# The second product of the second MLP with activations stationary: 512 weight columns moving, tokens on partitions

## The chip, the cores and the metric

The kernel runs on one core of a Trainium2 chip. The time is device microseconds of one execution; the figures given are the median of three runs and their spread. The trace is of one profiled execution, and its times count from the start of its span.

## What is computed

A trunk of two layers over 16 learned meta tokens and 256 real tokens, width 2048, all in float32: RWKV-7 time mixing, an MLP, gated linear attention (GLA), a second MLP, and a final norm. What the change touches is the end:

```python
def rms_norm(x, g, eps=NORM_EPS):
    y = x * lax.rsqrt(jnp.mean(x * x, axis=-1, keepdims=True) + eps)
    return y * g

def sq_relu_mlp(x, w1, w2):          # w1: 2048 x 8192, w2: 8192 x 2048
    h = jax.nn.relu(x @ w1)
    return (h * h) @ w2
...
    h = h + sq_relu_mlp(rms_norm(h, norm_mlp[i]), mlp_w1[i], mlp_w2[i])
return rms_norm(h, norm_f)[:, N_META:]
```

## The kernel before

The residual stream `hres` lies in SBUF as 128 partitions x 16 tiles x 272 tokens: features on partitions, tokens along the free axis. In the second MLP only the 256 real tokens are worked on.

**Weights.** They come from HBM in loads of 512 KB (128 partitions x 1024 float32), all issued on SP's queue (L132, tile `raw`, 3 buffers). Each is split in two: ScalarE casts it to a rounded part `hi` (L140), VectorE subtracts to get the rest `lo` (L141); `hi` and `lo` have 2 buffers each. These three steps carry a priority 2000 instructions ahead of their place in the program, so that the scheduler, which writes down a fixed order for each engine, puts them before other work that is ready at the same time. Activations are split in the same way. A product keeps hi x hi, hi x lo and lo x hi.

**Products.** A load holds 8 stationary tiles of 128x128. `projw` (L185 to L202) makes a pair of matmuls for each: behind the hi weights 512 columns move (256 tokens of the hi activations and 256 of the lo ones), behind the lo weights 256 columns (L196, L197). `mm3` (L163 to L165) does the same with three matmuls of 256 or 272 columns. The moving operand is read interleaved (`weave`). The result has features on partitions and accumulates in a PSUM bank of the tag `pj`, which has two banks. Other tags are `pm` (1), `pt` (2), `pry` (1) and `pu` (2).

**The MLP.** The hidden width 8192 is worked through in 4 blocks of 2048. `up(b)` makes 16 hidden tiles: a projection of 2 loads, the two halves joined (L206, L207), relu and scaling by the norm (L272), square (L275), split (L277, L278). `down(b)` projects the block onto 16 output tiles, 2 loads each, and two adds on VectorE put them into `hres` (L213). The order is up 0, up 1, down 0, up 2, down 1, up 3, down 2, down 3. The last output tile of the last block goes through `mm3`.

**The end.** While the last block goes down, `last` (L1307) squares each finished tile, sums the squares over tiles and multiplies the tile by `norm_f`. Then a product with ones sums over partitions (L1323), Ln and Exp give the norm's factor for each token (L231, L232), six products apply it, one of them on GpSimd (L1328), and six transfers on SP's queue write the output (L1330).

Two other places of the program serve as measures. At the start, 13 matmuls of 512 columns run on a constant tile, to have TensorE busy (L382). In the GLA and the RWKV layer, float32 transposes of 64 rows by 64 columns run in clusters on TensorE, two at a time on the two halves of the partitions (L1231, L745). L225 is a projection of plain float32 without a split.

Of the kernel before, what the change touches and what calls it, by code (L numbers as in the profile page):

```python
# [10 lines left out]
F32 = mybir.dt.float32  # L11
F32R = mybir.dt.float32r
AF = mybir.ActivationFunctionType
ALU = mybir.AluOpType
# [4 lines left out]
P = 128  # L19
D = 2048  # L20
KT = D // P
NMETA = 16
SEQ = 256
T = NMETA + SEQ
TP = 288
FF = 4 * D
NHB = FF // D
HEAD = 64
NG = 4
C = 64  # L30
NC4 = 4
DECAY = float(np.exp(-0.5))
NORM_EPS = 1e-6
# [13 lines left out]
GAPS = [(4, 2), (4, 2), (4, 2), (4, 3), (5, 5)]  # L47

MARK = [120, 170, 244, 302]

OUTQ = [0, 1, 4, 5]
OUTA = [4, 5, 6, 7, 12, 13, 14, 15]
# [2 lines left out]
class Kern:  # L55
# [203 lines left out]
    def mlp(self, layer, x, rstd, hres, off, done):  # L259
        nc, tc, ap = self.nc, self.tc, self.ap  # L260
        n = T - off
        w1, w2 = ap[f"mlp_w1_{layer}"], ap[f"mlp_w2_{layer}"]
        with ExitStack() as es:
            hp = es.enter_context(tc.tile_pool(name=f"hid{layer}", bufs=1, side="right", reuse_waits="tile"))

            def up(b):
                hid = []
                for f in range(KT):
                    src = [w1[b * KT + f, i] for i in range(2)]
                    ps = self.joined(hp, self.projw(src, x)) if n == SEQ else self.proj(src, x, n)  # L270
                    z = self.t(hp, [P, T], "z", 2)[:, :n]
                    nc.vector.scalar_tensor_tensor(out=self.two(z), in0=ps, scalar=0.0, in1=self.two(rstd), op0=ALU.max,  # L272
                                                   op1=ALU.mult)
                    s = self.t(hp, [P, T], "s", 2)[:, :n]
                    nc.scalar.activation(s, z, AF.Square)  # L275
                    ht = self.t(hp, [P, 2, T], "h", 2 * KT, F32R)
                    nc.scalar.copy(ht[:, 0, :n], s)  # L277
                    nc.vector.tensor_tensor(out=ht[:, 1, :n], in0=s, in1=ht[:, 0, :n].bitcast(F32), op=ALU.subtract)  # L278
                    hid.append(ht)
                return hid  # L280

            def down(b, hid):
                for f in range(KT):
                    src = [w2[f, 2 * b + i] for i in range(2)]
                    one = n != SEQ or (b, f) == (NHB - 1, KT - 1)
                    self.addto(hres[:, f, off:], [self.proj(src, hid, n)] if one else self.projw(src, hid))
                    if b == NHB - 1:
                        done(f)

            hid = up(0)  # L290
            for b in range(1, NHB):
                nxt = up(b)
                down(b - 1, hid)
                hid = nxt
            down(NHB - 1, hid)


    def rwkv(self, done):
# [228 lines left out]
        def scores(b, c, e):  # L527
            BK, AR = BKs[c > 1], ARs[c > 1]
            n, np = (C, 4) if c < NC4 else (32, 8)
            o = 128 * (c % 2) if c < NC4 else 256  # L530
            cs = slice(o, o + 2 * n)

            pv = [self.ptr().rearrange("p (h m) -> p h m", h=np)[: 2 * n, :, : 2 * n] for _ in range(2)]
            for p in range(np):
                for q in range(2):
                    rows = slice(64 * q, 64 * q + 64)
                    nc.tensor.matmul(pv[q][:, p], BK[rows, 4 * e + p, cs], AR[rows, 4 * e + p, cs], start=True, stop=True)
            dst, mk = (AMs[c > 1][:, c % 2, 8 * e : 8 * e + 8], self.maskA) if c < NC4 else (AMrs[0], self.maskR)
            for q in range(2):
                tt(dst[:, q::2], pv[q], mk.unsqueeze(1).to_broadcast([2 * n, np, 2 * n]))  # L540

            for rows, x in blocks(c, slice(8 * e, 8 * e + 8) if c < NC4 else slice(16)):
                with tc.high_priority(offset=4000):
                    nc.sync.dma_start(sysd[b][rows].rearrange("h s t -> s h t"), x)
# [418 lines left out]
        def until(n):  # L963
            R(n - ran[0])

        def some(it, n):
            for _ in range(n):
                next(it, None)
# [21 lines left out]
        with tc.manual_schedule(engines={ENG.PE}):  # L990
# [5 lines left out]
            for g in range(2):  # L996
                last = nothing
                if g:
# [7 lines left out]
                    last = norm(1)  # L1006
                until(MARK[2 * g])
                some(inv, 99)
# [19 lines left out]
                for c in range(5):  # L1028
                    if c == 2:
                        R(8)  # L1030
                        some(inv, 99)
                        if g == 0:
                            scores(2, 0, 0)
                        until(MARK[2 * g + 1])
                        m = merge(2 * g + 1)
# [243 lines left out]
@with_exitstack  # L1279
def trunk(ctx, tc, ap):  # L1280
    K = Kern(ctx, tc, ap)
    nc = tc.nc
    out, hres = ap["out"], K.hres
    st = {}

    def operand(gname, off, pool):
        def f(kt):
            if kt == 0:
                p = pool()
                st["x"] = [K.t(p, [P, 2, T], "x", KT, F32R) for _ in range(KT)]  # L1290
                st["acc"] = K.t(K.sp, [P, T], "acc")
            with tc.high_priority(offset=3000) if kt == KT - 1 else ExitStack():
                K.prep(K.sp, kt, hres[:, kt, off:], gname, st["x"][kt], st["acc"], T - off)
        return f

    def x2():
        K.x2p = K.sp = ctx.enter_context(tc.tile_pool(name="x2", bufs=1, side="right", reuse_waits="tile"))
        return K.x2p

    K.rwkv(operand("norm_mlp0", 0, x2))  # L1300
    rstd = K.accstd(K.sp, st["acc"], T)
    K.mlp(0, st["x"], rstd, hres, 0, operand("norm_mix1", 0, lambda: K.xp))
    rstd = K.accstd(K.sp, st["acc"], T)
    K.gla(st["x"], rstd, hres, operand("norm_mlp1", NMETA, lambda: K.xp))
    rstd = K.accstd(K.sp, st["acc"], SEQ)

    def last(kt):  # L1307
        if kt == 0:
            st["acc"] = K.t(K.sp, [P, T], "acc")
        h = hres[:, kt, NMETA:]  # L1310
        if kt < KT - 1:
            K.sqacc(K.sp, kt, h, st["acc"], SEQ)
        else:
            st["sq"] = K.t(K.sp, [P, T], "sq")[:, :SEQ]
            nc.scalar.activation(st["sq"], h, AF.Square)  # L1315
        nc.scalar.mul(h, h, K.vec("norm_f", kt))

    fp = ctx.enter_context(tc.tile_pool(name="fin", bufs=1, side="right"))
    fin = K.t(fp, [P, KT - 2, SEQ], "fin")
    K.mlp(1, st["x"], rstd, hres, NMETA, last)  # L1320
    ss = K.pm()[:, :SEQ]
    for i, x in enumerate((st["acc"][:, :SEQ], st["sq"])):
        nc.tensor.matmul(ss, K.ones, x, start=i == 0, stop=i == 1)  # L1323
    rstd = K.rstd_from(K.sp, ss, SEQ, 1.0 / D, NORM_EPS, "acc")
    for a, b in ((0, 1), (14, 16), (1, 3), (3, 6), (6, 10), (10, 14)):
        h = hres[:, a:b, NMETA:]
        y = fin[:, a:b] if b < KT else h
        (nc.gpsimd if b == KT else nc.vector).tensor_tensor(out=y, in0=h, in1=rstd.unsqueeze(1).to_broadcast([P, b - a, SEQ]),  # L1328
                                                           op=ALU.mult)
        nc.sync.dma_start(out[:, a:b], y)  # L1330


def _tiles(w):
    k, f = w.shape
    return np.ascontiguousarray(w.reshape(k // 1024, 8, P, f // P, P).transpose(3, 0, 2, 1, 4)).reshape(
        f // P, k // 1024, P, 1024)


def _pad(w, cols):
# [82 lines left out]
```

## Time and profile before

| | |
|---|---|
| median of 3 runs | 2378.53 us (2377.47 to 2379.18) |
| span of the profiled execution, its own time | 2375.3 us |
| TensorE matmuls busy | 2344.9 us, 19849 instructions |
| VectorE busy | 1607.3 us, 2701 instructions |
| ScalarE busy | 1259.7 us, 2005 instructions |
| moved by DMA | 449.20 MB |

The span runs from the first to the last instruction that the profiler recorded. Busy time is the time in which at least one instruction of the engine was under way; matmuls overlap each other, so a matmul's own duration is longer than the step from one to the next. PEld are the weight loads of TensorE. Register, branch, semaphore and DMA-issuing instructions are not counted as busy.

### The profile page before, as it was taken

The numbers are of one execution on the slowest core, as the hardware profiler recorded it, in microseconds if no ns is written. First come the engines' busy times: TensorE is split into PE (matmuls) and PEld (weight loads), VectorE is DVE, ScalarE is ACT, GpSimd is POOL, SyncE is SP. The second block draws the span as 40 slices with busy tenths as digits, with TensorE's granted clock in tenths as the row PEclk, the third lists the DMA queues.
The fourth block names the chain that finished last, engine by engine and source line by source line (L and its number), as shares of the span: only waits on it lengthen the run. The fifth ranks groups of instructions, "written<-read, shape, count | busy, mean of one in ns | idle before, by whom it ended". The sixth has DMA issues, their size and how long they took to land. (4 is left out here: it accounts for less than half of the span.)

```text
span 2375.3 us, 48373 instructions
## 1 busy us (share of the span) xinstructions
PE 2344.9 (99%) x19849; PEld 2224.1 (94%) x19849; DVE 1607.3 (68%) x2701; ACT 1259.7 (53%) x2005; POOL 13.6 (1%) x38
## 2 busy tenths in 40 slices
PE   9999999999999999999999999999999999999998
PEld 8888888889999999999999999999999999999997
DVE  8869986848555555555556777767666666666666
ACT  6478645566555345345345556645555445445444
POOL 0000000000000000000000000000000000000000
PEclk9999999999999999999999999999999999999999
DMA  6469754535555555555555655456565666666664
GB/s 214 155 198 310 245 159 145 144 98 180 186 192 189 188 194 187 189 192 188 190 191 190 199 175 174 162 168 202 179 203 200 200 203 200 200 203 200 199 204 169
DMA packets 157005, 449.20 MB, mean 189 GB/s; under 512 B 33968, under 2 KB 49968, under 8 KB 156784
## 3 DMA queue, kind: packets, MB, share of 16 engines
q1 hardware_dynamic: 156784, 446.11, 57.8%
q8 instruction: 156, 2.56, 0.5%
q14 instruction: 65, 0.53, 0.1%
HBM read 429.93 MB, written 14.42 MB: 187 GB/s over the span
## 5 line engine op out<-in xcount | busy, mean ns | idle before, releaser
L141 DVE TENSOR_TENSOR lo<-raw,hi 128x1024 fp32r<-128x1024 f32 (+1 forms) x818 | 927.4, 1140 | 532.9 <-ACT hi L140 523.1
L140 ACT CAST hi<-raw 128x1024 fp32r<-128x1024 f32 (+1 forms) x818 | 794.2, 978 | 918.8 <-PE pj L164 519.4
L163 PE MATMUL pj<-x,hi 128*128 128x272 f32 (+1 forms) x2560 | 728.1, 284 | 1.6 <-DVE r L300 0.9
L165 PE MATMUL pj<-x,lo 128*128 128x272 f32 (+1 forms) x2560 | 714.8, 279 | 5.1 <-DVE lo L141 5.0
L164 PE MATMUL pj<-x,hi 128*128 128x272 f32 (+1 forms) x2560 | 713.8, 279 | 0.5 <-DVE x L240 0.5
L163 PEld LDWEIGHTS pj<-x,hi 128*128 128x128 f32 x2560 | 484.8, 189 | 14.1 <-issue 6.5
L165 PEld LDWEIGHTS pj<-x,lo 128*128 128x128 f32 x2560 | 484.9, 189 | 7.8 <-DVE lo L141 7.5
L164 PEld LDWEIGHTS pj<-x,hi 128*128 128x128 f32 x2560 | 485.0, 189 | 3.2 <-issue 1.4
L196 PE MATMUL pj<-x,hi 128*128 128x512 f32 x1280 | 419.8, 382 | 0.1
L197 PE MATMUL pj<-x,lo 128*128 128x256 f32 x1280 | 348.7, 273 | 0.0
L196 PE MATMUL pj<-h,hi 128*128 128x512 f32 x1008 | 330.3, 382 | 0.0
L163 PE MATMUL pj<-h,hi 128*128 128x272 f32 (+1 forms) x1040 | 290.1, 279 | 0.0
L164 PE MATMUL pj<-h,hi 128*128 128x272 f32 (+1 forms) x1040 | 290.1, 279 | 0.0
L165 PE MATMUL pj<-h,lo 128*128 128x272 f32 (+1 forms) x1040 | 290.1, 279 | 0.0
L197 PE MATMUL pj<-h,lo 128*128 128x256 f32 x1008 | 274.9, 273 | 0.1
L196 PEld LDWEIGHTS pj<-x,hi 128*128 128x128 f32 x1280 | 241.9, 189 | 33.9 <-DVE x L1088 0.4
L197 PEld LDWEIGHTS pj<-x,lo 128*128 128x128 f32 x1280 | 245.8, 192 | 0.1
L196 PEld LDWEIGHTS pj<-h,hi 128*128 128x128 f32 x1008 | 190.5, 189 | 26.5
L163 PEld LDWEIGHTS pj<-h,hi 128*128 128x128 f32 x1040 | 196.6, 189 | 0.0
L164 PEld LDWEIGHTS pj<-h,hi 128*128 128x128 f32 x1040 | 196.6, 189 | 0.0
L165 PEld LDWEIGHTS pj<-h,lo 128*128 128x128 f32 x1040 | 196.6, 189 | 0.0
L197 PEld LDWEIGHTS pj<-h,lo 128*128 128x128 f32 x1008 | 193.5, 192 | 0.4 <-DVE lo L141 0.4
(283 smaller groups left out, 2171.5 us busy)
## 6 DMA issues: line engine op xcount, KB each, us to landing
raw<-mlp_w_d SPq DMA_DIRECT2D x512, 512.0 KB, 3.4
raw<-gla_in_d SPq DMA_DIRECT2D x98, 512.0 KB, 3.4
raw<-w_rkv_d SPq DMA_DIRECT2D x80, 512.0 KB, 4.1
raw<-gla_o_d SPq DMA_DIRECT2D x32, 512.0 KB, 3.3
raw<-w_r_d SPq DMA_DIRECT2D x16, 512.0 KB, 3.4
raw<-rw_oQ_d SPq DMA_DIRECT2D x16, 512.0 KB, 3.4
raw<-lora_d SPq DMA_DIRECT2D x8, 512.0 KB, 3.7
raw<-rw_oA_d SPq DMA_DIRECT2D x8, 512.0 KB, 4.2
```

The lines of the kernel that those rows point to most:

```text
L140: nc.scalar.copy(hi[:, h], raw[:, h])
L141: nc.vector.tensor_tensor(out=lo[:, h], in0=raw[:, h], in1=hi[:, h].bitcast(F32), op=ALU.subtract)
L163: nc.tensor.matmul(out, hi[:, ws], xh, start=first, stop=False)
L164: nc.tensor.matmul(out, hi[:, ws], xl, start=False, stop=False)
L165: nc.tensor.matmul(out, lo[:, ws], xh, start=False, stop=last)
L196: nc.tensor.matmul(wide, hi[:, ws], xt, start=kt == 0, stop=False)
L197: nc.tensor.matmul(one, lo[:, ws], xt[:, 0], start=False, stop=kt == nk - 1)
```

## The change

The second MLP has a function of its own, `mlp1`.

- **Order:** up 0, down 0, up 1, down 1, and so on; TensorE's order is that of the program.
- **Up:** as before, but two hidden tiles share one tile `H`, whose split (copy and subtraction) is made for both together, 512 elements wide.
- **Down:** the hidden activations are now the stationary operand (128 hidden features x 128 tokens), and 512 weight columns move. A pass has two halves (g = 0, 1) of 1024 output features. A half has 16 loads of 512 KB; each feeds 4 groups (2 halves of the tokens, t, by 2 blocks of 512 features, f) of three matmuls with 512 columns. The groups accumulate over the half in four banks: `pu`, `pu`, `pt`, `pt` for g = 0 and `pm`, `pry`, `pj`, `pj` for g = 1. With the last load each group is added into `htok` (256 tokens on partitions, 2048 features along the free axis). Loads go by turns to the old buffers and to a second set (2 `raw`, 2 `hi`, 2 `lo`).
- **Transposes:** behind each of the first 8 projections of up 0, four 128x128 float32 transposes on TensorE bring `hres` into `htok`, and ScalarE copies them out of PSUM.
- **norm_f** is loaded once as a broadcast over the partitions (1 MB), into memory of `hres`.
- **The end:** squares are summed along the free axis while ScalarE squares (`accum_out`), the factor of each token is one number per partition, and eight transfers of 256 KB write the output.
- The host lays out the weights of this product anew, with as many bytes and loads as before.

```diff
+    def mlp1(self, x, rstd):
...
+        pools = [self.wp, hp]
+        def load(src):
+            with tc.high_priority(offset=2000):
+                pool = pools.pop(0)
+                pools.append(pool)
+                raw = self.t(pool, [P, 1024], "raw", self.raw_bufs if pool is self.wp else 2)
+                hi = self.t(pool, [P, 1024], "hi", self.hi_bufs, F32R)
+                lo = self.t(pool, [P, 1024], "lo", self.hi_bufs, F32R)
+                nc.sync.dma_start(raw, src)
+                nc.scalar.copy(hi, raw)
+                tt(lo, raw, hi.bitcast(F32), ALU.subtract)
+                return hi, lo
+        def turn(i):
+            t, q = i // 4, i % 4
+            pt = self.ptr()
+            for j in range(4):
+                nc.tensor.transpose(pt[:, j * P : (j + 1) * P], hres[:, 4 * q + j, NMETA + P * t : NMETA + P * t + P],
+                                    self.ident)
+            nc.scalar.copy(htok[:, t, 512 * q : 512 * q + 512], pt)
...
+                nc.scalar.activation(F[:, 2 * k : 2 * k + 2].rearrange("p a t -> p (a t)"), z, AF.Square)
+                if b == 0 and f < 8:
+                    turn(f)
...
+                nc.scalar.copy(H[:, 0], F)
+                tt(H[:, 1], F, H[:, 0].bitcast(F32), ALU.subtract)
...
+        def final(t, q, late=False):
+            h, i = htok[:, t, 512 * q : 512 * q + 512], q
+            sq = self.t(hp, [P, 512], "fsq", 2)
+            nc.scalar.activation(sq, h, AF.Square, accum_out=ssq[:, t, i : i + 1])
+            if not late:
+                tt(h, h, nf[:, 512 * q : 512 * q + 512], ALU.mult)
+        def down(b, hid):
+            for g in range(2):
...
+                bank = [self.pu(), self.pu(), self.ptr(), self.ptr()] if g == 0 else [self.pm(), self.pry(), self.pj(), self.pj()]
+                for p in range(KT // 2):
+                    for k in range(2):
+                        hi, lo = load(ap["w2"][b, g, p][:, 2 * k : 2 * k + 2])
+                        for i, (t, f) in enumerate(((1, 0), (1, 1), (0, 0), (0, 1))):
+                            xh, xl = (hid[p][:, n, 2 * k + t] for n in range(2))
...
+                            nc.tensor.matmul(o, xh, self.weave(hi[:, ws]), start=first, stop=False)
+                            nc.tensor.matmul(o, xh, self.weave(lo[:, ws]), start=False, stop=False)
+                            nc.tensor.matmul(o, xl, self.weave(hi[:, ws]), start=False, stop=last)
+                            if last:
+                                tt(C[t, f], bank[i], C[t, f], ALU.add)
+                                if b == NHB - 1:
+                                    final(t, 2 * g + f, late=(g, f) == (1, 1))
+        with tc.manual_schedule(engines={mybir.EngineType.PE}):
+            for b in range(NHB):
+                hid = up(b)
+                if b == 0:
+                    nc.sync.dma_start(nf, ap["nf"].to_broadcast([P, D]))
+                down(b, hid)
...
+        for t, q in ((1, 3), (0, 3)):
...
+            tt(s3, ssq[:, t, others[0] : others[0] + 1], ssq[:, t, others[1] : others[1] + 1], ALU.add)
+            tt(s3, s3, ssq[:, t, others[2] : others[2] + 1], ALU.add)
+            nc.vector.tensor_scalar(out=s3, in0=s3, scalar1=1.0 / D, scalar2=NORM_EPS, op0=ALU.mult, op1=ALU.add)
+            nc.scalar.activation(rt[t], ssq[:, t, q : q + 1], AF.Ln, scale=1.0 / D, bias=s3)
+            nc.scalar.activation(rt[t], rt[t], AF.Exp, scale=-0.5)
...
+            nc.vector.scalar_tensor_tensor(out=h[:, c], in0=h[:, c], scalar=rt[t], in1=nf[:, c], op0=ALU.mult, op1=ALU.mult)
+            a, m, e = (slice(512 * i, 512 * i + 512) for i in others)
+            nc.scalar.mul(h[:, a], h[:, a], rt[t])
+            for y in (m, e):
+                nc.vector.tensor_scalar(out=h[:, y], in0=h[:, y], scalar1=rt[t], scalar2=None, op0=ALU.mult)
+            for y in (c, a, m, e):
+                nc.sync.dma_start(out[:, y], h[:, y])
...
-    K.mlp(1, st["x"], rstd, hres, NMETA, last)
-    ss = K.pm()[:, :SEQ]
-    for i, x in enumerate((st["acc"][:, :SEQ], st["sq"])):
-        nc.tensor.matmul(ss, K.ones, x, start=i == 0, stop=i == 1)
-    rstd = K.rstd_from(K.sp, ss, SEQ, 1.0 / D, NORM_EPS, "acc")
...
+    st["x2"].close()
+    K.mlp1(st["x"], rstd)
```

## Rows read from the trace of the kernel before

**Rows 1.** The page: span, and busy time of each engine.

```profile
span 2375.3 us, 48373 instructions
...
PE 2344.9 (99%) x19849; PEld 2224.1 (94%) x19849; DVE 1607.3 (68%) x2701; ACT 1259.7 (53%) x2005; POOL 13.6 (1%) x38
```

**Rows 2.** Busy time by stretch, second MLP: PE, PEld, DVE, ACT, POOL; clock, DMA share, GB/s.

```profile
1692.00:2363.30 671.30, 671.09 (x4112) 617.07 (x4111) 440.66 (x589) 344.46 (x480) 0.00 (x0) 1.00 0.60 198
```

**Rows 3.** The chain that ended last: start us, us; first and last of 31 in turn.

```profile
1735.82 0.22 PE pj L196
...
1740.73 0.22 PE pj L196
```

**Rows 4.** Timeline of PE from 12.05 us: start us, us, line, operation, shapes, count.

```profile
11.88 2.54 PE L382 MATMUL pu<-ar 128*128 128x512 f32 x11
```

**Rows 5.** Timeline of PE, last output tile: first and last of 48.

```profile
2357.97 0.28 PE L163 MATMUL pj<-h,hi 128*128 128x256 f32 x1
...
2363.22 0.28 PE L165 MATMUL pj<-h,lo 128*128 128x256 f32 x1
```

**Rows 6.** Timeline of PE, a cluster of transposes in the GLA.

```profile
1415.90 0.28 PE L165 MATMUL pj<-x,lo 128*128 128x272 f32 x1
1416.11 0.40 PE L1231 MATMUL pt<-cst,vs 64*128 64x64 f32 x6
...
1416.66 0.28 PE L164 MATMUL pj<-x,hi 128*128 128x272 f32 x1
1416.78 0.28 PE L165 MATMUL pj<-x,lo 128*128 128x272 f32 x1
```

**Rows 7.** Timeline of PE, transposes of the RWKV layer: second and seventh pair.

```profile
380.35 0.22 PE L745 MATMUL pt<-cst,BK 64*128 64x64 f32 x1
...
380.66 0.22 PE L745 MATMUL pt<-cst,BK 64*128 64x64 f32 x1
```

**Rows 8.** Groups by line and shape on PE: busy us, mean ns, idle before.

```profile
L225 PE MATMUL pj<-x,raw 128*128 128x272 f32 x128 | 29.7, 392 | 0.0
```

**Rows 9.** Groups by line and shape on DVE, whole span: busy us, mean ns.

```profile
L300 DVE TENSOR_TENSOR AM<-pt,cst 128x512 f32<-128x512 f32 x32 | 21.1, 681 | 6.3 <-PE pt L537 6.3
...
L240 DVE SCALAR_TENSOR_TENSOR x<-hres,vecs,x 128x256 fp32r<-128x256 f32 x16 | 7.7, 480 | 1.2 <-ACT x L239 1.2
...
L300 DVE TENSOR_TENSOR ar<-r,W 128x16 f32<-128x16 f32 x16 | 2.7, 168 | 0.0
...
L1179 DVE TENSOR_SCALAR KX<-KX,eb 128x64 f32<-128x64 f32 x8 | 2.0, 250 | 0.0
...
L1176 DVE TENSOR_SCALAR KX<-KX,eb 128x16 f32<-128x16 f32 x8 | 1.8, 229 | 0.0
```

**Rows 10.** Timeline of the tail: DVE's first add and the final products.

```profile
2363.53 0.42 DVE L213 TENSOR_TENSOR hres<-pj,hres 128x256 f32<-128x256 f32 x1 [2.83 <-PE pj L165]
...
2366.15 5.23 DVE L1328 TENSOR_TENSOR fin<-hres,acc 128x256 f32<-128x256 f32 x5 [2.19 <-ACT acc L232]
```

**Rows 11.** Timeline in an up pass; in brackets idle time before, and its releaser.

```profile
1748.29 1.23 DVE L141 TENSOR_TENSOR lo<-raw,hi 128x1024 fp32r<-128x1024 f32 x1 [0.60 <-ACT hi L140]
...
1749.83 1.05 ACT L140 CAST hi<-raw 128x1024 fp32r<-128x1024 f32 x1 [0.82 <-PE pj L196]
```

**Rows 12.** DMA issues: count, KB each, median us from issue to landing.

```profile
out_d<-fin SPq DMA_DIRECT2D x2, 512.0 KB, 2.8
...
BK<-bkd SPq DMA_DIRECT2D x1, 1280.0 KB, 8.2
...
out_d<-hres SPq DMA_DIRECT2D x1, 256.0 KB, 2.2
```

**Rows 13.** Timeline at the one late weight load: ACT, then PE.

```profile
2198.53 1.05 ACT L140 CAST hi<-raw 128x1024 fp32r<-128x1024 f32 x1 [1.99 <-DMA raw<-mlp_w_d]
...
2200.37 0.38 PE L196 MATMUL pj<-h,hi 128*128 128x512 f32 x1
2200.89 0.38 PE L197 MATMUL pj<-h,lo 128*128 128x256 f32 x1
```

More of the change, by code (lines that the diff above doesn't have):

```diff
@@ L295, in mlp, with up @@
             down(NHB - 1, hid)
+    def mlp1(self, x, rstd):
+        nc, tc, ap = self.nc, self.tc, self.ap
+        tt = lambda o, a, b, op: nc.vector.tensor_tensor(out=o, in0=a, in1=b, op=op)
+        w1, hres, rs = ap["mlp_w1_1"], self.hres, rstd[:, :SEQ]
+        es = ExitStack()
+        hp = es.enter_context(tc.tile_pool(name="hid1", bufs=1, side="right", reuse_waits="tile"))
+        htok = self.t(hp, [P, 2, D], "htok")
+        flat = hres.rearrange("p k t -> p (k t)")
+        nf = flat[:, :D]
+        ssq = self.t(hp, [P, 2, 4], "ssq")
+        sum3 = self.t(hp, [P, 2], "sum3")
+        pools = [self.wp, hp]
[17 more added lines that the diff above has]
+            nc.scalar.copy(htok[:, t, 512 * q : 512 * q + 512], pt)
+        def up(b):
+            out = []
+            for f in range(KT):
+                ps = self.joined(hp, self.projw([w1[b * KT + f, i] for i in range(2)], x))
+                z = self.t(hp, [P, SEQ], "z", 2)
+                nc.vector.scalar_tensor_tensor(out=self.two(z), in0=ps, scalar=0.0, in1=self.two(rs), op0=ALU.max,
+                                               op1=ALU.mult)
+                p, k = f // 2, f % 2
+                if k == 0:
+                    F = self.t(hp, [P, 4, P], "F", 2)
+                nc.scalar.activation(F[:, 2 * k : 2 * k + 2].rearrange("p a t -> p (a t)"), z, AF.Square)
+                if b == 0 and f < 8:
+                    turn(f)
+                if k == 0:
+                    continue
+                H = self.t(hp, [P, 2, 4, P], "H", KT // 2, F32R)
+                nc.scalar.copy(H[:, 0], F)
+                tt(H[:, 1], F, H[:, 0].bitcast(F32), ALU.subtract)
+                out.append(H)
+            return out
+        def final(t, q, late=False):
[6 more added lines that the diff above has]
+            for g in range(2):
+                C = {(t, f): htok[:, t, 1024 * g + 512 * f : 1024 * g + 512 * f + 512] for t in range(2) for f in range(2)}
+                bank = [self.pu(), self.pu(), self.ptr(), self.ptr()] if g == 0 else [self.pm(), self.pry(), self.pj(), self.pj()]
[4 more added lines that the diff above has]
+                            xh, xl = (hid[p][:, n, 2 * k + t] for n in range(2))
+                            ws, o = slice(512 * f, 512 * f + 512), self.pairs(bank[i])
+                            first, last = p + k == 0, p == KT // 2 - 1 and k == 1
+                            nc.tensor.matmul(o, xh, self.weave(hi[:, ws]), start=first, stop=False)
[11 more added lines that the diff above has]
+                down(b, hid)
+        rt = [self.t(hp, [P, 1], f"rt{t}") for t in range(2)]
+        for t, q in ((1, 3), (0, 3)):
+            others = [i for i in range(4) if i != q]
+            s3 = sum3[:, t : t + 1]
+            tt(s3, ssq[:, t, others[0] : others[0] + 1], ssq[:, t, others[1] : others[1] + 1], ALU.add)
[3 more added lines that the diff above has]
+            nc.scalar.activation(rt[t], rt[t], AF.Exp, scale=-0.5)
+            h = htok[:, t]
+            out = ap["out"][t]
+            c = slice(512 * q, 512 * q + 512)
+            nc.vector.scalar_tensor_tensor(out=h[:, c], in0=h[:, c], scalar=rt[t], in1=nf[:, c], op0=ALU.mult, op1=ALU.mult)
[5 more added lines that the diff above has]
+                nc.sync.dma_start(out[:, y], h[:, y])
+        es.close()
@@ L1296, in x2 @@
     def x2():
-        K.x2p = K.sp = ctx.enter_context(tc.tile_pool(name="x2", bufs=1, side="right", reuse_waits="tile"))
+        K.sp = ctx.enter_context(tc.tile_pool(name="sp", bufs=1, side="right", reuse_waits="tile"))
+        st["x2"] = ExitStack()
+        K.x2p = st["x2"].enter_context(tc.tile_pool(name="x2", bufs=1, side="right", reuse_waits="tile"))
         return K.x2p
@@ L1305, in trunk @@
     rstd = K.accstd(K.sp, st["acc"], SEQ)
[L1307 to L1319, printed above, removed]
-    K.mlp(1, st["x"], rstd, hres, NMETA, last)
-    ss = K.pm()[:, :SEQ]
-    for i, x in enumerate((st["acc"][:, :SEQ], st["sq"])):
-        nc.tensor.matmul(ss, K.ones, x, start=i == 0, stop=i == 1)
-    rstd = K.rstd_from(K.sp, ss, SEQ, 1.0 / D, NORM_EPS, "acc")
[L1325 to L1330, printed above, removed]
+    st["x2"].close()
+    K.mlp1(st["x"], rstd)
 def _tiles(w):
@@ L1336, in _tiles, with _blocks @@
         f // P, k // 1024, P, 1024)
+def _blocks(w):
+    w = w.reshape(NHB, KT // 2, 2, P, 2, 2, 256, 2).transpose(0, 4, 1, 3, 2, 5, 7, 6).reshape(NHB, 2, KT // 2, P, 4, 512)
+    return w
 def _pad(w, cols):
@@ L1400 @@
         arr[f"mlp_w1_{i}"] = _tiles(a["mlp_w1"][i])
-        arr[f"mlp_w2_{i}"] = _tiles(a["mlp_w2"][i])
+    arr["mlp_w2_0"] = _tiles(a["mlp_w2"][0])
+    arr["w2"] = _blocks(a["mlp_w2"][1])
+    arr["nf"] = np.ascontiguousarray(a["norm_f"]).reshape(1, D)
     win = a["gla_w_in"][0]
@@ L1415 @@
           for k, v in arr.items()}
-    ap["out"] = nc.dram_tensor("out_d", (P, KT, n), F32, kind="ExternalOutput").ap()
+    ap["out"] = nc.dram_tensor("out_d", (2, P, D), F32, kind="ExternalOutput").ap()
     with _tile.TileContext(nc) as tc:
@@ L1419 @@
     r = _run(nc, [{k + "_d": v for k, v in arr.items()}], core_ids=[0])
-    o = r.results[0]["out_d"].transpose(1, 0, 2).reshape(D, n).T
-    return np.ascontiguousarray(o)[None]
+    return np.ascontiguousarray(r.results[0]["out_d"]).reshape(1, n, D)
```

## Prediction

> **What bounds the kernel now.** I read the page first: span 2375.3 us, TensorE busy 99% of it, VectorE 68%, ScalarE 53% [rows 1]. That average could still hide a stage with another limit, so next the stretch of the second MLP alone: in 671.3 us TensorE is busy 671.09, the granted clock is 1.00 (2.4 GHz), VectorE 440.66, ScalarE 344.46 [rows 2]. Then the chain of waits through that stretch: it is nothing but L196 and L197, one behind the other [rows 3]. So here a nanosecond on TensorE is a nanosecond of the kernel, and work on the other engines counts only where TensorE has to wait for it. One more thing is to be seen before the change is costed: matmul durations overlap, so what counts is the distance from start to start.
>
> All sums are against this execution, span 2375.3 us. The median of the runs is 2378.5, 3.2 us more; I add the sum to the median.
>
> **1. The matmuls.** Each load of 512 KB fed 8 pairs: 512 columns behind the hi weights, 256 behind the lo weights. It now feeds 4 groups of three matmuls with 512 columns. Columns: 8 x 768 = 6144 before, 12 x 512 = 6144 after. So no work on the array is saved; only the cost of an instruction beyond its columns can be. In the chain 15 pairs take 1740.73 - 1735.82 = 4.91 us, 327.5 ns a pair [rows 3], 2620 ns a load. What a row of nothing but 512-column matmuls takes is shown by 13 warm-up matmuls near the start, with the same interleaved reading and a weight load for each: the last 11 span 2.54 us, the last of them lasts 0.38, so 10 steps take 2.16 us, 216 ns each [rows 4]. Twelve make 2592 ns. Where the missing time sat is seen in the last product before: 256-column matmuls with a load each go from 2357.97 to 2363.22 in 47 steps, 111.7 ns each, though 327.5 - 216 leaves the same 111.5 for the 256-column one in a pair [rows 5]: next to a 256-column stream a weight load does not quite fit, next to 512 it does. Saved 28 ns x 128 loads = 3.6 us, and 0.1 for the last column block (48 x 111.7 ns = 5.36 us against 5.24): **-3.7**. Bounds: -3.9 (512 columns at 215 ns) and 0 (512 at 218.3, two thirds of a pair). I take the 216, since these rows have exactly the new shape.
>
> **2. The transposes.** New on TensorE: 32 of 128x128 float32, in 8 clusters of 4, each between two projections of the first up pass. The nearest row is the cluster of 6 (64 rows, 64 columns) in the gated attention: L165 at 1415.90, L164 at 1416.66; less two slots of 0.12 (1416.66 to 1416.78) that leaves 0.52 us [rows 6]. Such transposes run two at a time, a pair every 62 ns (380.35 to 380.66 in five steps) [rows 7], so 0.19 us is streaming and 0.33 us is going into transposes and out of them: the neighbouring matmuls start late on either side. For a 128-column transpose I take 112 ns, the step of a back-to-back weight load of 128 columns [rows 5], since nothing overlaps it. A cluster: 4 x 0.112 + 0.33 = 0.78 us; eight: **+6.2**. Bounds: 62 ns each, 8 x 0.58 = 4.6; two passes of 109 ns each, as a plain float32 matmul of 272 columns shows them (29.7 us for 128 instructions, 0.85 ns a column), 8 x 1.20 = 9.6 [rows 8].
>
> Here a page speaks against the change. The Trainium skill, "TensorE: Matmul & The Clock Gate", section "Part 4: PE-mode transpose", gives a 128x128 transpose some 275 ns in a kernel's context. By that the term would be an estimated 32 x 0.275 = 8.8 us in place of 6.2, and the forecast 2387.0. The 0.22 us in [rows 7] come near it as a duration, but a pair follows every 62 ns there, so I do not take it as a step.
>
> **3. From a down pass back to the next up pass.** This is the new wait. The second half of a down pass (g = 1) accumulates in pm, pry and both pj banks, and the next up pass begins with the first of those pj banks. It has to wait for the add that empties it, the third of four. Let the last load of the pass start at 0 on TensorE. Its four groups end at 0.65, 1.30, 1.94, 2.59. An add of 128x512 out of PSUM takes 0.68 us on VectorE [rows 9]. The first runs from 0.65 + 0.2 (the lag of L213 behind the last matmul [rows 5, 10]) to 1.5. By then the lo split of the second load of the up pass is ready: its hi buffer was freed at 0, ScalarE's cast takes 1.05 [rows 11], so at 1.2. It carries the higher priority, so it goes next, 1.23 us, to 2.8; the second add ends at 3.5, the third at 4.2. TensorE wanted the bank at 2.59: 1.65 us idle, three times: **+5.0**. Queued behind the matmul that waits is all of TensorE; nobody else is late, since casts and splits run ahead. Bounds: if the splits stand behind the adds, three adds in a row end at 2.9, 3 x 0.4 = 1.2; if the split stands before all adds, 4.5, 3 x 2.0 = 6.0. Between the halves of a pass, and from up to down, the banks have long been emptied, and in a down pass four hi/lo buffers in place of two carry TensorE through the adds: zero. If that cover fails, a late lo costs what it did at 2200 us (part 4).
>
> **4. The load of norm_f.** A broadcast of 1 MB on SP's queue, in front of weight loads; a 1280 KB transfer took 8.2 us to land [rows 12]. What one late weight load costs is to be seen once: ScalarE's cast at 2198.53 had waited 1.99 us for its transfer, the lo weights came late in turn, and from the L196 at 2200.37 to the L197 behind it went 0.52 us in place of 0.22, with 0.10 more behind that [rows 13]. I take one such: **+0.4**; bounds 0 (it meets the down pass with its five raw buffers) and 3.
>
> **5. Elementwise work.** The up pass keeps its rhythm; only the copy and subtraction of the hidden block come once for 512 elements. Before its splits VectorE is idle at least 0.60 us, ScalarE 0.82 before its casts [rows 11]; 0.26 more (0.68 less 0.42) on either fits. Eight copies of 512 columns out of PSUM, no longer than an add of that size [rows 9], run in the 0.78 us that TensorE spends on a cluster. The 64 x 2 adds of L213 become 32 adds of 0.68. All hidden: 0. The end of the gated attention is the same.
>
> **6. The tail.** Removed: the sum over partitions (two calls, 4 matmuls), square, Ln and Exp over 256 columns, six products with VectorE and GpSimd [rows 10]. The last L165 starts at 2363.22, so the matmuls end at 2363.33 [rows 5]. VectorE ended at 2366.15 + 5.23, 8.05 us after the last matmul, and the span 3.95 us after that. New, on VectorE from 1.74 us before the last matmul ends (the first of the last four groups ends 1.94 before it, and 0.2 of lag): 4 adds and 2 products by norm_f of 0.68 (4.1), six tiny sums of 0.168 (1.0), two scalar_tensor_tensor of 512 (0.48 for 256 by L240, so 0.75 each: 1.5), four tensor_scalar of 512 (250 ns at 64 columns, 229 at 16: 0.44 ns a column, 0.45 each: 1.8) [rows 9]. That is 8.4, ending 6.7 after the last matmul. The squares, Ln and Exp on ScalarE lie beside it. The last transfer is 256 KB, landing in 2.2 us against 2.8 for 512 KB [rows 12], so the end is 3.35 behind VectorE: 10.0 us against 12.0, **-2.0**. Bounds: -3.0 (the tiny sums all fall into gaps before the last add) and 0 (VectorE waits 2 us for the second row statistic).
>
> **Sum:** -3.7 + 6.2 + 5.0 + 0.4 - 2.0 = +5.9: 2378.5 + 5.9 = **2384.4 us**, 0.25% slower. All lows together: -3.9 + 4.6 + 1.2 + 0 - 3.0 = -1.1; all highs: 0 + 9.6 + 6.0 + 3.0 + 0 = +18.6.
>
> **Rivals.** (a) The adds stand before the splits on VectorE, so that term 3 costs 1.2: the sum is +2.1, 2380.6 us, no change. For it: the adds come earlier in time than the split at an ideal pace; against: the split is ready before the second add. It decides where the wait falls under 1.3 us per pass: then the sum is below +4.8 us. (b) The transposes take two passes: +9.3, 2387.8 us. For: plain float32 products pay twice a column [rows 8]; against: six transposes stand as six instructions in [rows 6]. (c) The wide matmuls gain nothing, 218.3 ns each: +9.5, 2388.0 us; against it are [rows 4]. (d) Faster by more than 4.8 us: none of my lows reaches it, it would need a saving on TensorE that no row shows.
>
> **Chances.** Less than 0.2% (4.8 us) is about what a measurement here cannot tell from no change. Forecast 0.46 (of it 0.07 under the 0.2%), (a) 0.28, (b) 0.13, (c) 0.06, (d) 0.07. So slower 0.58, same 0.35, faster 0.07. Range 2377 to 2390: from just under (a) with the short tail and low transposes to just above (b) and (c).
>
> **What would show it.** After: 512-column matmuls of the down pass 216 ns apart; eight gaps of 0.8 us around the transposes in the first 50 us of the second MLP; three idle stretches of TensorE of about 1.6 us, each put down to a VectorE add, with a lo split just before it; 10 us from the last matmul to the end. Wrong would be: no such idle stretch (then a), 1.2 us per cluster (b), 218 ns (c), or idle time of TensorE at other places, which I have not seen coming.

## The result, and the profile after

After the change the kernel takes 2382.80 us (median of 20 runs, 2380.09 to 2383.78); before, 2379.03 on the same chips (20 runs, 2377.47 to 2381.12). The ratio of the runs is 1.0014, 95% interval 1.0008 to 1.0021: 3.3 us slower, 1.9 to 5.0 (the two medians lie 3.8 us apart). The forecast was 2384.4 us, 0.25% slower, with a range of 2377 to 2390. The direction is right and the time lies in the range; but 0.14% is under the 0.2% that the prediction itself set as the bound of "same", an outcome to which it gave 0.35 against 0.58 for slower.

That the sum came out near does not say that its terms did. So the trace is read term by term. The page of the changed kernel, to be held against [rows 1]:

```profile
span 2381.5 us, 47187 instructions
...
PE 2346.8 (99%) x19349; PEld 2209.9 (93%) x19349; DVE 1567.3 (66%) x2573; ACT 1249.7 (52%) x1969; POOL 12.1 (1%) x37
```

500 fewer matmuls, and TensorE is busy 1.9 us more: as foretold, there was no work on the array to be saved. The span is 6.2 us longer in these two profiled executions, but 2.4 of that lies ahead of any changed instruction. The sum over partitions of the norm ahead of the second MLP stands at the same place of both programs and starts at 1693.85 us before and 1696.25 after:

```profile
1693.85 0.70 PE L255 MATMUL pm<-acc,cst 128*128 128x256 f32 x2
```

```profile
1696.25 0.70 PE L256 MATMUL pm<-acc,cst 128*128 128x256 f32 x2
```

In the eight experiments below, whose code is the same up to there, that point lies anywhere from 1693.85 to 1696.50. It scatters from execution to execution, and I leave it out by measuring everything from that matmul. From it to the end of the last matmul of the MLP it is 2363.33 - 1693.85 = 669.48 us before and 2369.33 + 0.22 - 1696.25 = 673.30 after: **+3.8**. Behind the MLP's last matmul come 12.0 us before and 2381.5 - 2369.55 = 11.95 after: **0.0**.

PE's timeline in a down pass, and at one cluster of transposes of the first up pass (start us, us, line, operation, count):

```profile
1784.81 0.38 PE L372 MATMUL pu<-lo,H 128*128 128x512 f32 x1
...
1796.46 0.38 PE L372 MATMUL pt<-lo,H 128*128 128x512 f32 x1
```

```profile
1699.62 0.27 PE L198 MATMUL pj<-x,lo 128*128 128x256 f32 x1
1699.73 0.60 PE L328 MATMUL pt<-cst,hres 128*128 128x128 f32 x4
1700.09 0.46 PE L197 MATMUL pj<-x,hi 128*128 128x512 f32 x1
1700.38 0.27 PE L198 MATMUL pj<-x,lo 128*128 128x256 f32 x1
```

Between the first two lines lie 54 steps in 11.65 us: 215.7 ns each (215.9 over other stretches), just the 216 taken from the warm-up matmuls [rows 4]. Twelve make 2590.5 ns a load against 2620 before. In the second fence, from one L198 to the next it is 0.76 us where a pair takes 0.327: a cluster costs 0.43, not the 0.78 of the forecast. Two things are to be seen in it: the first transpose starts 0.11 behind the L198 ahead of it, as any matmul would, and four take 0.36 (1699.73 to 1700.09; they start 109 ns apart), while a single one is shown with 273 ns. Durations overlap; starts count.

What TensorE waited for from 1690 us on (line, releaser: us in total, times, longest), and how one of the three waits comes about: the engines from 1862.4 us on, in order of time.

```profile
PE pj L197 <- DVE htok L301: 3.8, 3, 1.3
```

```profile
1862.49 1.05 ACT L141 CAST hi<-raw 128x1024 fp32r<-128x1024 f32 x1 [1.54 <-PE pj L373]
...
1863.14 0.69 DVE L301 TENSOR_TENSOR htok<-pm,htok 128x512 f32<-128x512 f32 x1 [0.93 <-PE pm L373]
...
1863.75 1.22 DVE L142 TENSOR_TENSOR lo<-raw,hi 128x1024 fp32r<-128x1024 f32 x1
...
1864.67 0.38 PE L373 MATMUL pj<-hi,H 128*128 128x512 f32 x1
1864.88 0.68 DVE L301 TENSOR_TENSOR htok<-pry,htok 128x512 f32<-128x512 f32 x1
...
1865.48 0.68 DVE L301 TENSOR_TENSOR htok<-pj,htok 128x512 f32<-128x512 f32 x1
...
1866.31 0.46 PE L197 MATMUL pj<-x,hi 128*128 128x512 f32 x1 [1.26 <-DVE htok L301]
...
1866.60 0.27 PE L198 MATMUL pj<-x,lo 128*128 128x256 f32 x1
```

VectorE empties pm, then turns to the lo split of the next up pass (ready when the cast ends at 1863.54), then empties pry and the first pj bank, at 1866.16. TensorE's last matmul of the down pass started at 1864.67 and its next slot was 1864.89; it starts at 1866.31. That is 1.43 us idle, and 0.07 more in the pair behind (L197 to L198 0.29 instead of 0.22): 1.50, three times 4.5.

Put together: matmuls -3.8 and -0.1, transposes 8 x 0.43 = +3.5, the wait +4.5, a lo half that came late near 1745 us +0.2, and -0.4 for the late weight load of before [rows 13], which this execution does not have. That is +3.9 against +3.8 measured. The -0.4 can't be put down to the change: seven of the nine profiled kernels with the changed code have no such load in this stretch, another, the last experiment, has two.

The tail, on VectorE and SP's queue (8 issues in one line), then by the microsecond (from:to, us, busy PE, PEld, DVE, ACT, POOL, clock, DMA share, GB/s):

```profile
2369.33 0.38 PE L373 MATMUL pj<-hi,H 128*128 128x512 f32 x1
...
2372.49 0.75 DVE L397 SCALAR_TENSOR_TENSOR htok<-htok,rt,hres 128x512 f32<-128x512 f32 x1 [0.57 <-ACT rt L393]
...
2373.24 4.47 SPq L403 DMA_DIRECT2D out_d<-htok  x8
...
2374.61 0.88 DVE L401 TENSOR_SCALAR htok<-htok,rt 128x512 f32<-128x512 f32 x2
```

```profile
2373.00:2374.00 1.00, 0.00 (x0) 0.00 (x0) 1.00 (x4) 0.82 (x2) 0.00 (x0) 0.50 0.00 0
2374.00:2375.00 1.00, 0.00 (x0) 0.00 (x0) 1.00 (x3) 0.00 (x0) 0.00 (x0) 0.50 0.93 342
...
2378.00:2379.00 1.00, 0.00 (x0) 0.00 (x0) 0.00 (x0) 0.00 (x0) 0.00 (x0) 0.50 1.06 402
2379.00:2380.00 1.00, 0.00 (x0) 0.00 (x0) 0.00 (x0) 0.00 (x0) 0.00 (x0) 0.50 0.78 295
2380.00:2381.00 1.00, 0.00 (x0) 0.00 (x0) 0.00 (x0) 0.00 (x0) 0.00 (x0) 0.50 0.00 0
```

VectorE ends at 2375.49, 5.9 us behind the last matmul, sooner than the 6.7 foretold. But the end comes 6.0 us behind VectorE, not 3.35. From 2374 to 2380 the DMA engines do nothing but carry the 2.1 MB of output, at 295 to 402 GB/s with a share near 1. From 2380 to the end of the span nothing is shown to move and no engine to work. The first transfer was issued 3.7 us behind the last matmul's end; before it was 3.3 (2366.66 less 2363.33), and from there to the end it took 8.7 us with six transfers, against 8.3 now with eight of the same bytes in all:

```profile
2366.66 0.34 SPq L1330 DMA_DIRECT2D out_d<-fin  x1
```

### The profile page after: what moved, and what is told of

Same layout as the page of the kernel before. It is cut to its first block, busy times and chain, and to the rows that moved or that the text cites. A ratio compares the mean times of both kernels' runs of the same rounds, so it can differ in the third digit from the quotient of the medians.

```text
span 2381.5 us, 47187 instructions
## 1 busy us (share of the span) xinstructions
PE 2346.8 (99%) x19349; PEld 2209.9 (93%) x19349; DVE 1567.3 (66%) x2573; ACT 1249.7 (52%) x1969; POOL 12.1 (1%) x37
## 5 line engine op out<-in xcount | busy, mean ns | idle before, releaser
L142 DVE TENSOR_TENSOR lo<-raw,hi 128x1024 fp32r<-128x1024 f32 (+1 forms) x690 | 770.4, 1124 | 449.8 <-ACT hi L141 445.2
L141 ACT CAST hi<-raw 128x1024 fp32r<-128x1024 f32 (+1 forms) x690 | 659.8, 965 | 738.2 <-PE pj L165 520.2
L197 PE MATMUL pj<-x,hi 128*128 128x512 f32 x1280 | 421.3, 383 | 3.9 <-DVE htok L301 3.8
L198 PE MATMUL pj<-x,lo 128*128 128x256 f32 x1280 | 348.9, 273 | 0.0
L166 PE MATMUL pj<-h,lo 128*128 128x272 f32 x1024 | 285.8, 279 | 0.0
L164 PE MATMUL pj<-h,hi 128*128 128x272 f32 x1024 | 285.7, 279 | 0.0
L165 PE MATMUL pj<-h,hi 128*128 128x272 f32 x1024 | 285.7, 279 | 0.0
L197 PEld LDWEIGHTS pj<-x,hi 128*128 128x128 f32 x1280 | 241.9, 189 | 38.6 <-ACT hi L320 4.9
L301 DVE TENSOR_TENSOR lo<-raw,hi 128x1024 fp32r<-128x1024 f32 x128 | 156.8, 1225 | 144.1 <-ACT hi L320 144.1
L198 PEld LDWEIGHTS pj<-x,lo 128*128 128x128 f32 x1280 | 245.7, 192 | 0.3 <-DVE lo L142 0.2
L320 ACT CAST hi<-raw 128x1024 fp32r<-128x1024 f32 x128 | 134.2, 1048 | 184.5 <-PE pt L373 91.1
L166 PEld LDWEIGHTS pj<-h,lo 128*128 128x128 f32 x1024 | 193.5, 189 | 0.0
L164 PEld LDWEIGHTS pj<-h,hi 128*128 128x128 f32 x1024 | 193.5, 189 | 0.0
L165 PEld LDWEIGHTS pj<-h,hi 128*128 128x128 f32 x1024 | 193.5, 189 | 0.0
L214 DVE TENSOR_TENSOR hres<-pj,hres 128x272 f32<-128x272 f32 (+1 forms) x96 | 41.8, 436 | 44.0 <-PE pj L166 36.9
L273 DVE SCALAR_TENSOR_TENSOR z<-pj,acc 128x272 f32<-128x272 f32 x64 | 28.3, 442 | 38.2 <-PE pj L166 38.2
```

The source lines that it names most:

```text
L141: nc.scalar.copy(hi[:, h], raw[:, h])
L142: nc.vector.tensor_tensor(out=lo[:, h], in0=raw[:, h], in1=hi[:, h].bitcast(F32), op=ALU.subtract)
L164: nc.tensor.matmul(out, hi[:, ws], xh, start=first, stop=False)
L165: nc.tensor.matmul(out, hi[:, ws], xl, start=False, stop=False)
L166: nc.tensor.matmul(out, lo[:, ws], xh, start=False, stop=last)
L197: nc.tensor.matmul(wide, hi[:, ws], xt, start=kt == 0, stop=False)
```

## Experiments

In what follows "the stretch" is the time from the norm's sum matmul to the start of the MLP's last matmul (673.08 us after the change), and "the tail" the time from there to the end of the span (12.17 us). Times of runs stand beside runs of the kernel before on the same chip. Two experiments leave work out or write less; their expectations say which.

**The order of the banks.** Is the wait made by the bank that the up pass takes first, or would TensorE have waited there for VectorE anyway?

```diff
-bank = ... if g == 0 else [self.pm(), self.pry(), self.pj(), self.pj()]
+bank = ... if g == 0 else [self.pj(), self.pj(), self.pm(), self.pry()]
```

> Second half of each down pass accumulates in pj, pj, pm, pry instead of pm, pry, pj, pj; nothing else. Theory W (TensorE waits at the start of an up pass for the add that empties the first pj bank, which stands third and behind a lo split): the first group now goes to that bank, its add ends 1.5 us into the last load, before TensorE wants the bank at 2.6. The three idle stretches of 1.43 us (and 0.07 each in the next pair) vanish: 4.5 us less than the changed kernel, about 2378.3 us, ratio to before 0.9997. Rival V (the stretches come from VectorE being late with the bunch of four adds and a split, whatever the bank): the stretch moves to the first lo weights of the up pass and stays at 1 us or more each, ratio 1.001 or above.

2378.29 us (11 runs, 2376.05 to 2381.08), ratio to before 0.9996 (0.9988 to 1.0005). The stretch is 668.59 us, 4.49 less, which is the 4.5 read off above. The three steps go by without a wait, while VectorE does the same things in the same order, add, split, add (PE, then DVE):

```profile
1862.70 0.38 PE L373 MATMUL pry<-hi,H 128*128 128x512 f32 x1
1862.92 0.38 PE L197 MATMUL pj<-x,hi 128*128 128x512 f32 x1
```

```profile
1861.18 0.69 DVE L301 TENSOR_TENSOR htok<-pj,htok 128x512 f32<-128x512 f32 x1 [0.93 <-PE pj L373]
...
1861.79 1.22 DVE L142 TENSOR_TENSOR lo<-raw,hi 128x1024 fp32r<-128x1024 f32 x1
...
1862.92 0.68 DVE L301 TENSOR_TENSOR htok<-pj,htok 128x512 f32<-128x512 f32 x1
```

The bank that is wanted next is emptied at 1861.87, before the split. So VectorE was not too slow here; the next pass asked for a bank that it emptied third.

**No transposes.** The hidden state is not turned.

```diff
+nc.gpsimd.memset(htok, 0.0)
...
-if b == 0 and f < 8:
-    turn(f)
```

> The eight clusters of transposes and their copies are left out and htok is set to zero, so the residual is missing from the output. Theory (read from the trace after: a cluster costs 4 x 109 ns with next to nothing for going in and out, 0.433 us): 3.5 us less than the changed kernel, 2379.3. Rival (the clusters cost what the prediction said, 0.78 us each, part of it hidden in later pairs): 6.2 us less, 2376.6.

The stretch is 669.57 us, 3.51 less: 0.44 a cluster, as in the trace, and not the 0.78 of the forecast. The time is 2379.07 us (10 runs), ratio 1.0 (0.9991 to 1.0009). The tail, whose code is the same, is 12.58 us in the profiled execution: it scatters by some 0.4.

**Each transpose as two of 64 rows.** Where did the 0.33 us for going into transposes and out of them come from, the transposing or the half rows of [rows 6, 7]?

```diff
-    nc.tensor.transpose(pt[:, j * P : (j + 1) * P], hres[:, 4 * q + j, ...], self.ident)
+    for e in range(2):
+        r = slice(HEAD * e, HEAD * e + HEAD)
+        nc.tensor.transpose(pts[e][:, j * HEAD : (j + 1) * HEAD], hres[r, 4 * q + j, ...], self.ident[r, r])
```

> Each 128x128 transpose is made as two of 64 rows, each into a bank of its own, two copies in place of one: the form from which the prediction took its 0.33 us per cluster. Theory H (that cost belongs to instructions on half of the rows, not to transposes): a cluster costs 4 x 62 ns + 0.33 = 0.58 us in place of 0.433, and gaps of 0.1 us or more stand before and behind it. Rival F (the cost in the attention came from waits there): a cluster costs 0.25 us to 0.33 us, without gaps.

A single run, 2384.39 us. PE's timeline at the same cluster:

```profile
1699.45 0.27 PE L198 MATMUL pj<-x,lo 128*128 128x256 f32 x1
1699.65 0.46 PE L331 MATMUL pt<-cst,hres 64*128 64x64 f32 x8
1700.05 0.48 PE L197 MATMUL pj<-x,hi 128*128 128x512 f32 x1
1700.37 0.27 PE L198 MATMUL pj<-x,lo 128*128 128x256 f32 x1
```

From L198 to L198 now 0.92 us: a cluster costs 0.59 instead of 0.43, and the stretch is 674.10 us, 1.0 longer (eight clusters make some 1.2; the lo half that came late near 1745 us, 0.2, is on time here). The gaps are back: 0.20 from L198 to the first transpose where 128 rows took 0.11, and 0.32 from L197 to L198 where 0.29 stood. Four pairs at 62 ns and 0.33 make 0.58, so the sum made from [rows 6, 7] is right for half rows. It was carried over to full ones, where it does not hold. Why half rows cost this at their edges is not shown, nor that the rows alone do it: the transposes here also move 64 columns instead of 128.

**256 columns at a time.** 24 matmuls per load instead of 12, with the same products.

```diff
+for v in range(2):
+    u = slice(128 * v, 128 * v + 128)
...
-nc.tensor.matmul(o, xh, self.weave(hi[:, ws]), ...)
+nc.tensor.matmul(o[:, u], xh, self.weave(hi[:, ws])[:, u], ...)
```

> Down passes with 24 matmuls of 256 columns per load in place of 12 of 512; same columns, same activations, same order of weights. Theory L (a weight load of 128 columns takes 111.7 ns and does not fit beside 256 columns): 24 x 111.7 = 2681 ns a load in place of 2590, 128 loads: 11.6 us slower than the changed kernel, 2394. Rival I (each matmul costs 2.6 ns beyond its columns, whatever its length): 24 x 109.3 = 2623, 4.2 us slower, 2387.

A single run, 2392.36 us: span 2390.2, stretch 684.49, 11.4 longer. In PE's timeline ten steps take 1.12 us:

```profile
1788.87 0.28 PE L376 MATMUL pu<-hi,H 128*128 128x256 f32 x1
...
1789.99 0.28 PE L374 MATMUL pt<-hi,H 128*128 128x256 f32 x1
```

112 ns each, so two cost 224 where one of 512 costs 216. The rival, 2.6 ns for each matmul whatever its length, would have made 4.2 us. So a 256-column matmul with a weight load of its own costs some 4 ns more than half of a 512-column one, and this is what the change's one gain rests on. That the load is what does not fit beside 256 columns is argued, not shown: the transposes have a load of 128x128 each too, and start 109 ns apart.

**Two queues for the output.** If the tail is long because SP issues eight transfers one behind the other, half of them on ScalarE's queue shorten it.

```diff
-for y in (c, a, m, e):
-    nc.sync.dma_start(out[:, y], h[:, y])
+for y, q in ((c, nc.sync), (a, nc.scalar), (m, nc.sync), (e, nc.scalar)):
+    q.dma_start(out[:, y], h[:, y])
```

> The changed kernel with four of its eight output transfers issued from ScalarE's queue instead of SP's; banks as in the changed kernel. Theory T (transfers bound by their 2.1 MB, 6 us): no change, within 0.3 us of the changed kernel, 2382.8, tail 12.0 us. Rival S (one queue issues eight transfers at about 0.5 us each, 3.9 us from the first issue to the last): the last issue comes some 1.5 us earlier and so does the end, tail 10.5 us, 2381.3.

2381.85 us (11 runs, 2380.42 to 2382.71), ratio 1.0011 (1.0002 to 1.002). The last issue comes 1.6 us earlier (6.19 us behind the last matmul's start instead of 7.77), the tail is 12.18 us, as before the edit. So the time that issuing takes is not what sets the end.

**Fewer outputs.** Of the first half of the tokens only one block is written.

```diff
-for y in (c, a, m, e):
+for y in (c, a, m, e) if t else (c,):
```

> The changed kernel, without three of the eight output transfers (the first three feature blocks of token half 0 are not written); all products are still made. Theory T: 1.3 MB in place of 2.1 MB, 2.2 us less to transfer: tail 10 us in place of 12.1, counted from the start of the last matmul. Rival S (VectorE's last product sets the end): tail unchanged.

A single run, 2380.39 us: tail 10.45 us, 1.7 less, with VectorE ending where it did (6.16 us behind the last matmul's start in both). Three transfers of 256 KB at 400 GB/s would be 2.0. So most of each transfer stands in the tail; this supports the transfers as its limit.

**Banks, and the end begun earlier.** If the first transfer sets the end, then forming the statistics of the first finished half of the tokens before the other half is added moves the end with it. On top of the order of banks, shortened (the products by norm_f of the third block of features are also folded into the last products):

```diff
-final(t, 2 * g + f, late=(g, f) == (1, 1))
+final(t, 2 * g + f, late=g == 1)
+if g == 1 and f == 1:
+    fin(t)          # row statistics, products and four transfers of this half
```

> pj banks first as in the run above, and in the last block the row statistic, Ln, Exp, products and transfers of token half 1 are written down right behind its second group, before the groups of token half 0; the products by norm_f of the third feature block are folded into the final scalar_tensor_tensor. Theory T (the tail is the wait for the first output plus the transfer of 2.1 MB at about 350 GB/s, 6.0 us, plus 1.7 us): the first output transfer is issued about 2 us earlier, so the tail shrinks from 12.0 to about 10 us and the kernel to about 2376.3 us, ratio 0.9988. Rival S (the end is set by VectorE's last product or by the issue of the last transfer on SP's queue): the last product moves by less than 0.7 us, so does the end.

2376.87 us (11 runs, 2375.64 to 2378.38), ratio to before 0.9991 (0.9982 to 1.0). First transfer and end both come some 0.9 us earlier (2.95 instead of 3.91 behind the last matmul's start; tail 11.25). The end moved with the first transfer, but by half of what I had expected. ScalarE's timeline says why:

```profile
2366.30 0.63 ACT L356 ACTIVATE fsq<-htok 128x512 f32<-128x512 f32 x1
...
2366.93 0.46 ACT L367 ACTIVATE rt<-ssq,sum 128x1 f32<-128x1 f32 x2
```

The squares of the other half went ahead, and both Ln stand together behind them.

**The end in order.** With the order of banks as above, the last down step's adds, squares, Ln, Exp and products written out in a fixed order for VectorE and ScalarE, and the sums of the blocks that are finished early formed early (shortened):

```diff
+with tc.manual_schedule(engines={E.PE, E.DVE, E.Activation}):
+    add(0, 1, 0); final(1, 2, late=True)
+    add(1, 1, 1); final(1, 3, late=True)
+    third(1); fin(1)
+    add(2, 0, 0); final(0, 2, late=True)
+    add(3, 0, 1); final(0, 3, late=True)
+    write(1); third(0); fin(0); write(0)
```

> As the run with the pj banks first and the early end, but VectorE's and ScalarE's order at the end is written out by hand: both squares of token half 1, its Ln and Exp and its first product stand before the squares of token half 0, and the sums of the first two feature blocks are formed in the half before. Theory T (tail = wait for the first output, plus some 8 us for 2.1 MB): the first output is issued about 1.3 us earlier than in the early-end run (1.7 us behind the start of the last matmul in place of 2.95), the tail falls from 11.2 us to about 10, the kernel to about 2375.6 us, ratio 0.9986. Rival S (the end is set by VectorE's last product, or by the last issue on SP's queue): VectorE's last product is no earlier, the tail stays at 11.2 us.

2375.48 us (11 runs, 2374.39 to 2377.85) beside 2378.85 of the kernel before, ratio **0.9986** (0.9977 to 0.9995): 3.4 us faster than before, and the lowest of all versions here. By the bound of 0.2% this too is "same", though the interval excludes 1. The span is 2373.4 us, the last matmul starts at 2363.42, so the tail is 10.0. The Ln of the first half now starts at 2364.02, and the first transfer goes out 1.73 us behind the last matmul's start:

```profile
2364.02 0.29 ACT L375 ACTIVATE rt<-ssq,sum 128x1 f32<-128x1 f32 x1
...
2364.65 0.47 DVE L384 TENSOR_SCALAR htok<-htok,rt 128x512 f32<-128x512 f32 x1
...
2365.15 4.46 SPq L388 DMA_DIRECT2D out_d<-htok  x8
```

```profile
2366.00:2367.00 1.00, 0.00 (x0) 0.00 (x0) 0.52 (x2) 0.88 (x4) 0.00 (x0) 1.00 1.03 373
...
2371.00:2372.00 1.00, 0.00 (x0) 0.00 (x0) 0.00 (x0) 0.00 (x0) 0.00 (x0) 0.50 0.69 262
```

From the first issue to the end it is 8.27 us here, 8.26 in the changed kernel (2381.5 - 2373.24), 8.31 in the step before this one. Over all eight kernels with the eight transfers it lies between 8.07 (256 columns) and 8.62 (no transposes), six of them within 0.05 of 8.3. No run here made it shorter with these bytes; what was moved is its start.

The stretch of this execution is 669.57 us, 1.0 longer than with the order of banks alone. The code of the loads is the same, but two weight loads came late (ScalarE's waits for transfers in the stretch, then PE at the second):

```profile
ACT hi L141 <- DMA raw<-mlp_w_d: 4.1, 2, 2.3
```

```profile
2259.07 0.38 PE L197 MATMUL pj<-x,hi 128*128 128x512 f32 x1
2259.91 0.38 PE L198 MATMUL pj<-x,lo 128*128 128x256 f32 x1 [0.45 <-DVE lo L142]
```

Why they were late is not shown.

## Why the prediction came out as it did

- **Matmuls, -3.7: right**, -3.8 and -0.1, and no work on the array was saved, as said: the gain is in the cost of an instruction beyond its columns. The weight load that "does not quite fit" beside 256 columns is in keeping with the 256-column run (112 ns a step), but not shown by it. The Trainium skill, "TensorE: Matmul & The Clock Gate", section "Wait — 56ns, not 53.3ns?", gives 215.7 ns for 512 columns at the higher clock; the trace agrees, with 215.7 to 215.9 ns at a granted clock of 1.00.
- **Transposes, +6.2: the streaming right, the edges wrong.** They cost 3.5. The step that failed was "0.33 us is going into transposes and out of them", read off clusters of half rows. With full rows there is no gap ahead of the cluster, and 0.08 behind it. The 112 ns for one transpose came out near, at 109, but its reason (a weight load that nothing overlaps) is not shown: one float32 instruction of [rows 8], at 0.85 ns a column, makes 109 for 128 columns as well. The trace of before had a nearer row for it, which the prediction passed over: the float32 matmuls of L732, with all 128 rows and 128 moving columns, start a pair every 109 ns (from 325.70 us). The 275 ns of the Trainium skill, "TensorE: Matmul & The Clock Gate", section "Part 4: PE-mode transpose", set aside in the prediction, are near what the trace shows as a duration (273 ns) and not as a step; 8.8 us for the term is refuted by the run without transposes.
- **From down to up, +5.0: right** in place, order and nearly in size, 4.5. (By the prediction's own times, 4.2 - 2.59, the wait is 1.61 and not 1.65, and 2.9 - 2.59 in its low bound 0.3 and not 0.4; the term would read +4.8.) The order add, split, add, add is the one worked out, and rival (a), adds first, is refuted by the timeline. Rivals (b) and (c) fall with the 0.43 us and the 216 ns.
- **norm_f, +0.4: not seen.** Its transfer landed in 5.5 us, and no cast of the stretch waited for a transfer. The step "I take one such" late load failed. The late load of before is missing too, which was not foreseen and is scatter as far as the runs show.
- **Elementwise, 0: nearly right.** The profile names no other wait of TensorE than the three. But the one late lo half of the stretch, near 1745 us, belongs here: its cast on ScalarE (1743.05) stood behind a square that had waited 1.32 us for VectorE. It cost 0.2.
- **Tail, -2.0: wrong**, 0.0. The step that failed is "so the end is 3.35 behind VectorE". It priced the last transfer as if it stood alone. Eight transfers together keep the DMA engines busy for 6 us, and the end followed the first issue by 8.07 to 8.62 us in eight kernels. VectorE's shorter work lies under that. So the removed work of [rows 10] was worth nothing: the first transfer went out 0.4 us later than before, and from there to the end it took 0.4 less.

The errors of the terms were +2.7 (transposes), +0.5 (wait), +0.6 (late loads and the late lo half: +0.4 foretold, 0.2 - 0.4 found), +0.2 (matmuls) and -2.0 (tail). They partly cancel, and +5.9 became +3.8 in the trace and +3.3 in the runs. That the total came out so near is in part luck: the tail's error hid most of the transposes'.

## What to carry to other kernels

When a new accumulation starts right behind an old one, let it take the bank that is emptied first: one line was worth all of the 4.5 us. A price taken from rows of another shape (here half of the partitions) is an estimate that an experiment has to check. A tail that ends in many transfers is priced from the first issue and the bytes; bring the first transfer forward, and only then shorten the arithmetic.

## What the runs showed of the hardware

- Transposes of 64 rows between full matmuls cost some 0.15 us a cluster more than the same data in 128-row transposes (0.59 against 0.43). They stream in less time (four pairs at 62 ns against four steps of 109); what is more lies at the edges.
- In the microseconds that the output filled, it left at 318 to 404 GB/s with one queue issuing the transfers (the changed kernel and the last experiment) and at 336 to 381 with two, and an issue on SP grew from 0.34 to 0.61 us while transfers were queued. The Trainium skill, "DMA: Bandwidth & Descriptors", section "Issuing engines are not separate DMA queues", says that transfers from several engines share the same 16 DMA engines; the tail of 12.18 us against 12.17 agrees.
- The point where the norm ahead of the second MLP begins moved by up to 2.65 us between profiled executions of kernels that are the same up to there (1693.85 to 1696.50). Compared from zero, such a trace would show an effect that is none.
- Late weight loads come and go in the same way: one in the execution before (0.4 us), none in most of the others, two in the last experiment (1.0 us).
